# A hybrid attention and MLP block: the product with w_out read in single PSUM banks, its weighing on VectorE, two low parts by adding DMAs

## The chip, the cores and the metric

The kernel runs on one core of a Trainium2 chip. The metric is the device time of one execution in microseconds. A core has a matrix engine (TensorE, here PE), a vector engine (VectorE, DVE), a scalar engine (ScalarE, ACT), a general engine (GpSimd, POOL) and a queue engine (SyncE, SP) that issues most transfers. PE writes its results into PSUM, which has eight banks; one bank holds 128 x 512 float32. Everything else lies in SBUF, and the large arrays in DRAM. The engines run on their own and wait for each other by semaphores.

## The reference

One block of a network over 1024 tokens of 1024 channels: two linear attention branches, merged by gates, then a product with `w_out`, a norm and a residual sum, then a second norm and an MLP. What the change touches begins with `merged`:

```python
merged = jax.nn.sigmoid(m_a) * y_a + jax.nn.sigmoid(m_d) * y_d
x = x + gate1 * rms_norm(merged @ w_out, post_mix_w)

h2 = rms_norm(x, pre_mlp_w) * (1.0 + scale2) + shift2
y = jnp.square(jax.nn.relu(h2 @ mlp_w1)) @ mlp_w2
x = x + gate2 * rms_norm(y, post_mlp_w)
```

All of it is float32.

## The kernel before, in words

*Products.* A float32 operand is split into a high part (rounded to the type fp32r, by a copy on ACT) and a low part (the operand less its high part, by a subtraction on DVE). A product is three matmuls: high by high, high by low, low by high. Every matmul is 128 x 128 by 128 x 512. The large products are made by Winograd's form of Strassen's method: the operands are cut into four quadrants, and seven products P1 to P7 of sums of quadrants take the place of eight. The sums of the results are had by letting several products accumulate in the same PSUM bank, with reads in between.

*The product with w_out* (from `out_plan`, line 1752) multiplies `merged` (quadrants Z11 to Z22, tiles `U`, `z` and `xq`) by `w_out` (quadrants B11 to B22, tiles `wq` and `raw`). The seven products run in the order P2, P1, P6, P5, P3, P7, P4. Each has four banks j of 128 tokens; in each bank k runs over four slices of the inner dimension, the first two of pair 0 (`kp`), the last two of pair 1. So a product is 4 x 4 x 3 = 48 matmuls, 12 a bank, and one "tick" of the kernel's clock is 6 matmuls, half a bank. The high and low parts are `mH`, `mL` (of `merged`) and `wO` (of `w_out`); `a_cast`, `b_cast` make the high parts, `a_low`, `b_low` the low ones.

*PSUM.* Two pools share the eight banks: `pm` has two tiles of two banks each (`pmt()`), `pa` four tiles of one bank (`pat()`). P2 fills two `pm` tiles, P1 to P3 then two more (the same two buffers, when P2's have been read), P7 and P4 four `pa` tiles. The results are gathered in tiles `y`: P2's is copied by ACT (`copy_y`), P1's is added to it by DVE (`first_half`); that is the first column half of the first token half. The sums after P6 and P5 are copied for the second token half; the sum after P3 is the first token half's second column half (`second_half`). P7 and P4 are added into the copies (`add_y`).

*The norm behind it.* For each token half: `square` takes the sums of squares on ACT, `weigh` multiplies a gathered 128 x 1024 tile by a weight row `gw1` (the norm's weight times gate1; tile `gw`) on GpSimd, `norm1` works out the factor in eleven short DVE operations, `residual` adds the scaled rows to x (tiles `xr`), `square2` and `norm2` are the same for the second norm, and give `xh`. `turn` transposes `xh` on PE into a `pm` tile and scales it on ACT into the tiles `F`. Both token halves do this, the second one during pass 1.

*Pass 1* is the start of the MLP: 32 products `prod1` of 12 matmuls each, of the weight w1 (tiles `w`, loaded to `raw`) by the first half's `F` (split into `oB`), into banks `pa`.

*What sets the order.* The code hands each engine its instructions in a fixed order. Calls of `at`, `on` and `st` put an operation at a tick: `on(t, ...)` means t ticks after P2's start. An operation stands in its engine's queue where its tick comes due in the program, and runs when its inputs and its buffer are ready and what stands ahead of it is done; it may run long before its tick. So a tick sets an order, not a time. The tiles `wO` and `w` lie in eight buffers (`wt`), so that a cast waits for PE to finish with an older weight.

The profile gives line 38, where a helper records every operation, for all of them: they are told apart by their tiles.

Of the kernel before, what the change touches and what calls it, by code (L numbers as in the profile page):

```python
# [8 lines left out]
F32 = mybir.dt.float32  # L9
# [3 lines left out]
AF = mybir.ActivationFunctionType  # L13
ALU = mybir.AluOpType
# [36 lines left out]
def block_kernel(ctx: ExitStack, tc: tile.TileContext, x, c, ada_w, ada_b, pre_mix_w, post_mix_w,  # L51
# [28 lines left out]
    def pmt():  # L80
        return pm.tile([128, 1024], F32, tag="pm", name=nm("pm"))
# [1321 lines left out]
    def on(t, fn):  # L1403
        at(begin + t - clock[0], fn)
# [159 lines left out]
    def r2(ps):  # L1564
        return ps.rearrange("p (a b) -> p a b", a=2)
# [305 lines left out]

    def turn(hf, a, g):

        pt = pmt()
        for i in range(4):
            for e in range(2):
                T.transpose(pt[:, i * 256 + e * 128:i * 256 + e * 128 + 128],
                            xhs[4 * hf + a + e][:, (4 * g + i) * 128:(4 * g + i + 1) * 128], ident)
        for i in range(4):
            k = 4 * g + i  # L1880
            if F[hf][k // 2] is None:
                F[hf][k // 2] = pair_tile("F")
            A.activation(F[hf][k // 2][:, k % 2, a * 128:(a + 2) * 128], pt[:, i * 256:(i + 1) * 256], AF.Identity,
                         scale=am2[:, k:k + 1], bias=sh2[:, k:k + 1])

    NG = 16
# [94 lines left out]
    on(64, lambda: norm1(1, 0, 4))  # L1981
    for j in range(4):
        on(64 + j, lambda j=j: residual(1, j, 0))
        on(66 + j, lambda j=j: square2(1, j))
    on(71, lambda: norm2(1, 0, 4))
    for n in range(4):
        on(74 + n, lambda n=n: turn(1, n // 2 * 2, n % 2))

    psb, psc = None, None
    for p in ("P2", "P1", "P6", "P5", "P3", "P7", "P4"):  # L1990
        if p in ("P2", "P1"):
            psb = [pmt(), pmt()]
        elif p == "P7":
            psc = [pat() for _ in range(4)]
        for h in range(2):
            if p == "P1":
                at(5 + 4 * h, lambda h=h, ps=psb: first_half(h, ps[h]))
            elif p in ("P2", "P6", "P5"):
                key = {"P2": (0, 0, h), "P6": (1, 0, h), "P5": (1, 1, h)}[p]
                at(5 + 4 * h, lambda h=h, ps=psb, key=key: copy_y(key, ps[h]))  # L2000
        for j in range(4):
            if p == "P3":
                at(3 + 2 * j, lambda j=j, ps=psb: second_half(j, four(ps)[j]))
            elif p in ("P7", "P4"):
                at(3 + 2 * j, lambda j=j, ps=psc, c=int(p == "P7"): add_y((1, c, j // 2), j, ps[j]))
        out_product(p, psc if p in ("P7", "P4") else four(psb), p in ("P2", "P1", "P7"))


    def t_ops():
# [76 lines left out]
    for n, (g, k) in enumerate(PASS1):  # L2086
        if n + 2 < len(PASS1):
            prep_pass1(*PASS1[n + 2], 0)
        if n % 2 and n // 2 + 4 < NG:
            at(0, lambda n=n: load_pass1(n // 2 + 4))  # L2090
        if n == 22:
            load_pass2(0, [t4((128, 4, 256), p="raw", tag="sl") for _ in range(2)])
        elif n in (27, 30):
            at(0, lambda n=n: load_pass2(1 if n == 27 else 2))
        if n == 26:
            p0 = prep_pass2(0)
            for j in range(8):
                at(j, p0[j])
        if n == 30:
            p1 = prep_pass2(1)  # L2100
            for j in range(4):
                at(j, p1.pop(0))
        if n < 30:
            at(0, lambda: some(1))
            if n % 2:
                at(1, lambda: some(1))
        if n == len(PASS1) - 1:
            load_uy(0)
        if k == 0:
            acc1[g] = pat()  # L2110
            uy1[g] = pair_tile("uy", "sl" if 4 <= g < 10 and g % 3 else "w4")
# [348 lines left out]
```

## Time and profile before

| | |
|---|---|
| median of 3 runs | 1912.64 us (1911.64 to 1913.68) |
| the profiled execution | 1912.39 us |
| its span, from the first to the last instruction | 1910.6 us |
| mean granted clock of PE | 0.995 |
| busy: PE, DVE, ACT, POOL | 98%, 73%, 46%, 9% |

The span is divided into busy time of each engine; a matmul counts as busy with a modelled end, so that PE can be busy and still lose time at a low clock. The product with w_out starts at 1178.1 us of the span, pass 1 at 1275.1 us. The timeline lists the instructions of one engine in order of time, like ones merged, with the idle time before one in brackets and the operation that ended it.

### The profile page before, as it was taken

The page shows a single profiled execution, that of the slowest core. Times are in us where ns is not written, and L with a number is a line of the kernel's source. Part 1 is how long each engine was busy: PE and PEld are TensorE (multiplying, and loading weights), DVE is VectorE, ACT ScalarE, POOL GpSimd, SP SyncE. Part 2 cuts the span into 40 slices and gives each one's busy share as a digit, 9 for nine tenths or more (in the row PEclk, how much of TensorE's full clock was granted, in tenths as well). Part 3 has the DMA queues.
Part 4 walks back from the last instruction along what each step waited for, and adds up shares of the span by engine and source line. Part 5 has one row for each costly group of instructions (what it writes and reads, how often), then busy time and mean ns, then how long its engine had stood idle before and what let it go on. Part 6 is the DMA issues. An engine that isn't in the chain of part 4 may idle for free. (4 is left out here: it accounts for less than half of the span.)

```text
span 1910.6 us, 26421 instructions
## 1 busy us (share of the span) xinstructions
PE 1871.3 (98%) x10169; PEld 1567.8 (82%) x10169; DVE 1386.7 (73%) x2129; ACT 887.3 (46%) x1609; POOL 163.0 (9%) x140
## 2 busy tenths in 40 slices
PE   7999999999999999999999999889999999999998
PEld 5788888989888888888888888668888888888886
DVE  5664834968756666766788679976678786777887
ACT  5564324243333444444655653558644446433333
POOL 2120111010110000000101100120012120000001
PEclk9999999999999999999999999989999999999999
DMA  9695573223125444444957853326666758252425
GB/s 312 216 252 185 153 144 101 78 78 111 56 85 175 131 131 131 131 131 160 231 180 188 257 149 112 93 87 222 223 208 216 249 204 307 96 220 90 175 99 99
DMA packets 251230, 309.07 MB, mean 162 GB/s; under 512 B 72450, under 2 KB 178128, under 8 KB 251104
## 3 DMA queue, kind: packets, MB, share of 16 engines
q1 hardware_dynamic: 222464, 274.67, 45.1%
q0 software_dynamic: 12368, 17.70, 5.3%
q10 hardware_dynamic: 16272, 15.02, 2.4%
q8 instruction: 80, 1.31, 0.3%
q14 instruction: 46, 0.38, 0.1%
HBM read 226.95 MB, written 80.39 MB: 161 GB/s over the span
## 5 line engine op out<-in xcount | busy, mean ns | idle before, releaser
L38 PE MATMUL pm<-hH,wH 128*128 128x512 f32 x864 | 286.7, 413 | 0.0
L38 PE MATMUL pm<-hL,wH 128*128 128x512 f32 x864 | 268.6, 392 | 0.0
L38 PE MATMUL pm<-hH,wL 128*128 128x512 f32 x864 | 267.4, 391 | 0.0
L38 PE MATMUL pm<-oH,wB 128*128 128x512 f32 x672 | 214.5, 394 | 0.0
L38 PE MATMUL pa<-w,yH 128*128 128x512 f32 (+1 forms) x696 | 212.3, 387 | 0.0
L38 PEld LDWEIGHTS pm<-hL,wH 128*128 128x128 f32 x864 | 162.2, 188 | 36.5
L38 PEld LDWEIGHTS pm<-hH,wL 128*128 128x128 f32 x864 | 162.1, 188 | 36.4
L38 DVE TENSOR_TENSOR w<-raw,w 128x512 fp32r<-128x512 f32 (+1 forms) x144 | 129.3, 901 | 46.7 <-ACT w L38 46.1
L38 PEld LDWEIGHTS pm<-hH,wH 128*128 128x128 f32 x864 | 145.1, 190 | 17.0
L38 PEld LDWEIGHTS pa<-w,yH 128*128 128x128 f32 x696 | 130.1, 188 | 26.8 <-DVE ya L38 0.4
L38 PEld LDWEIGHTS pm<-oH,wB 128*128 128x128 f32 x672 | 126.2, 188 | 25.7
L38 ACT CAST w<-raw 128x512 fp32r<-128x512 f32 (+1 forms) x144 | 99.4, 711 | 88.6 <-DVE raw L38 79.4
L38 PE MATMUL pa<-w,yL 128*128 128x512 f32 (+1 forms) x348 | 134.5, 387 | 0.0
L38 PE MATMUL pm<-oL,wB 128*128 128x512 f32 x336 | 130.9, 390 | 0.0
L38 PE MATMUL pa<-oB,w 128*128 128x512 f32 x480 | 113.8, 395 | 5.0 <-DVE w L38 5.0
L38 PEld LDWEIGHTS pa<-oB,w 128*128 128x128 f32 x480 | 90.8, 190 | 25.0 <-DVE w L38 6.2
L38 ACT CAST wH<-raw 128x1024 fp32r<-128x1024 f32 x62 | 64.5, 1048 | 98.3 <-PE pm L38 55.9
L38 DVE SCALAR_TENSOR_TENSOR cv<-pm,ccol,cv 128x1023 f32<-128x1023 f32 (+2 forms) x72 | 92.1, 1279 | 13.7 <-ACT cv L38 12.3
L38 DVE TENSOR_TENSOR wL<-raw,wH 128x1024 fp32r<-128x1024 f32 x62 | 76.1, 1231 | 34.8 <-ACT wH L38 34.7
L38 PE MATMUL pm<-oT,w 128*128 128x512 f32 x384 | 90.8, 389 | 0.0
L38 PE MATMUL pa<-oT,w 128*128 128x512 f32 x384 | 90.8, 389 | 0.0
L38 DVE TENSOR_TENSOR ya<-pa,ya 128x512 f32<-128x512 f32 (+1 forms) x83 | 56.0, 683 | 43.6 <-PE pa L38 43.6
(398 smaller groups left out, 3759.5 us busy)
## 6 DMA issues: line engine op xcount, KB each, us to landing
yL<-y_d SPq DMA_DIRECT2D x53, 512.0 KB, 7.2
raw<-in_mlp_w_dram SPq DMA_DIRECT2D x23, 1024.0 KB, 6.3
raw<-in_w_in_dram SPq DMA_DIRECT2D x18, 1024.0 KB, 7.3
raw<-in_w_in_dram SPq DMA_DIRECT2D x32, 512.0 KB, 5.0
araw<-in_ada_w_dram SPq DMA_DIRECT2D x32, 512.0 KB, 3.8
raw<-in_mlp_w_dram SPq DMA_DIRECT2D x18, 512.0 KB, 5.6
araw<-in_ada_w_dram SPq DMA_DIRECT2D x32, 256.0 KB, 6.8
sl<-sg_d SPq DMA_DIRECT2D x16, 512.0 KB, 6.9
```

Source lines behind the costliest of these rows:

```text
L38: r = fn(*args, **kw)
```

## The change

Five things are changed, all between P2 of the product with w_out and the middle of pass 1:

- `weigh` runs on VectorE instead of GpSimd; of the first token half it stands ten ticks (h = 0) and eight ticks (h = 1) later.
- P2 has two `pm` tiles of its own (`psa`); P1, P6, P5 and P3 accumulate in four `pa` tiles (`psb`), P7 and P4 in two `pm` tiles (`psc`). So P1 and P3 are read bank by bank, P6 and P5 copied in two halves, and P7 and P4 added as 128 x 1024 instead of 128 x 512.
- The low parts of P2's and P1's weights are made as in `b_neg`: ACT writes the negative high part, and a DMA of GpSimd's queue adds the quadrant of w_out from DRAM.
- `turn` works on a `pa` tile: four transposes into one bank and two scalings, twice as many calls. The first half's stand 4 ticks (first pair) and 2 ticks (second pair) later, its splits 2 ticks; of the second half, the norm stands 2 to 6 ticks later and the transposes 5.
- In `out_plan` the sums Z12 and Z21 stand 3 and 5 ticks later, and some casts and low parts of P5 and P4 a tick or two off. The transposed sums of the MLP come 4 ticks later, and `uy` tiles use the pool `sl` from g = 7 instead of 4.

```diff
+    def b_neg(p, key, kp):
+        H, L = ww[p, kp]
+        A.activation(L, H.bitcast(F32), AF.Copy, scale=-1.0)
+        r0 = key[0] * 512 + kp * 256
+        G.dma_start(L, w_out[r0:r0 + 256, HALF[key[1]]].rearrange("(k p) c -> p k c", p=128), accum_op=ALU.add)
...
-                  (-11 + 4 * kp, b_cast, "P2", B21, kp), (-10 + 4 * kp, b_low, "P2", B21, kp),
+                  (-11 + 4 * kp, b_cast, "P2", B21, kp), (-10 + 4 * kp, b_neg, "P2", B21, kp),
...
-                  (-3 + 4 * kp, b_cast, "P1", B11, kp), (-2 + 4 * kp, b_low, "P1", B11, kp),
+                  (-3 + 4 * kp, b_cast, "P1", B11, kp), (-2 + 4 * kp, b_neg, "P1", B11, kp),
...
-                  (12 + kp, a_sum, Z12, Z12, Z11, kp), (14 + kp, a_sum, Z21, Z22, Z11, kp),
-                  (14 + kp, a_cast, "P5", "s1", kp), (16 + kp, a_low, "P5", "s1", kp),
+                  (15 + kp, a_sum, Z12, Z12, Z11, kp), (19 + kp, a_sum, Z21, Z22, Z11, kp),
+                  (13 + kp, a_cast, "P5", "s1", kp), (17 + kp, a_low, "P5", "s1", kp),
...
-        tt(G, y, y, gw1[:, HALF[c]].unsqueeze(1).to_broadcast([128, 2, 512]), mul)
+        tt(V, y, y, gw1[:, HALF[c]].unsqueeze(1).to_broadcast([128, 2, 512]), mul)
...
-        pt = pmt()
-        for i in range(4):
+        pt = pat()
+        for i in range(2):
...
-    def first_half(h, ps):
-        tt(V, Y[0, 0, h], r2(ps), Y[0, 0, h], add)
+    def first_half(j, ps):
+        y = Y[0, 0, j // 2][:, j % 2]
+        tt(V, y, ps, y, add)
...
+    def add_y(c, h, ps):
+        y = Y[1, c, h]
+        tt(V, y, r2(ps), y, add)
...
-        on(16 + 4 * h, lambda h=h: weigh(0, 0, h))
+        on(26 + 2 * h, lambda h=h: weigh(0, 0, h))
...
-    for a, t in ((0, 45), (2, 51)):
-        for g in range(2):
-            on(t + g, lambda a=a, g=g: turn(0, a, g))
+    for a, t in ((0, 49), (2, 53)):
+        for g in range(4):
+            on(t + g // 2, lambda a=a, g=g: turn(0, a, g))
...
-    for n in range(4):
-        on(74 + n, lambda n=n: turn(1, n // 2 * 2, n % 2))
+    for n in range(8):
+        on(79 + n // 2, lambda n=n: turn(1, n // 4 * 2, n % 4))
...
-    psb, psc = None, None
+    psa, psb, psc = [pmt(), pmt()], None, None
     for p in ("P2", "P1", "P6", "P5", "P3", "P7", "P4"):
-        if p in ("P2", "P1"):
-            psb = [pmt(), pmt()]
+        if p == "P1":
+            psb = [pat() for _ in range(4)]
         elif p == "P7":
-            psc = [pat() for _ in range(4)]
+            psc = [pmt(), pmt()]
```

How the order moves is seen at three places of DVE's queue. The first is the gather of the first half, at the end of P1 and the start of P6. Before (`wO` and `mL` are low parts for P6 and P5, `y` the gathered tile, `z` and `U` sums of quadrants of merged):

```order
L38 TENSOR_TENSOR wO_10621<-wq_10585,wO_10620 128x1024
L38 TENSOR_TENSOR wO_10634<-wq_10598,wO_10633 128x1024
L38 TENSOR_TENSOR z_9207<-z_9207,U_8740 128x1024
L38 TENSOR_TENSOR z_9262<-z_9262,U_8811 128x1024
L38 TENSOR_TENSOR y_10577<-pm_10612,y_10577 128x1024
L38 TENSOR_TENSOR U_8992<-U_9102,U_8740 128x1024
L38 TENSOR_TENSOR U_9048<-U_9144,U_8811 128x1024
L38 TENSOR_TENSOR mL_10666<-xq_10538,mH_10665 128x1024
L38 TENSOR_TENSOR mL_10679<-xq_10567,mH_10678 128x1024
L38 TENSOR_TENSOR y_10624<-pm_10613,y_10624 128x1024
```

With the change:

```order
L38 TENSOR_TENSOR wO_10627<-wq_10589,wO_10626 128x1024
L38 TENSOR_TENSOR wO_10640<-wq_10602,wO_10639 128x1024
L38 TENSOR_TENSOR y_10581<-pa_10616,y_10581 128x512
L38 TENSOR_TENSOR y_10581<-pa_10617,y_10581 128x512
L38 TENSOR_TENSOR z_9207<-z_9207,U_8740 128x1024
L38 TENSOR_TENSOR y_10630<-pa_10618,y_10630 128x512
L38 TENSOR_TENSOR z_9262<-z_9262,U_8811 128x1024
L38 TENSOR_TENSOR mL_10663<-xq_10541,mH_10662 128x1024
L38 TENSOR_TENSOR y_10630<-pa_10619,y_10630 128x512
```

The two gathers of 128 x 1024 have become four of 128 x 512, and the sums that stood ahead of the first one now stand behind it.

The second place is the start of P4, behind the first half's norm (`xh` is its result, `wO` the last low part for P4, `y` the results of P7, `cw` the next pair's norm). Before:

```order
L38 TENSOR_SCALAR xh_10873<-xr_10590,rs_10988 128x1024
L38 TENSOR_SCALAR xh_10889<-xr_10610,rs_10988 128x1024
L38 TENSOR_TENSOR wO_10966<-wq_10307,wO_10965 128x1024
L38 TENSOR_TENSOR y_10820<-pa_10941,y_10820 128x512
L38 TENSOR_TENSOR y_10820<-pa_10942,y_10820 128x512
L38 TENSOR_SCALAR cw_11068<-vb_10504 128x2
```

With the change:

```order
L38 TENSOR_SCALAR xh_10885<-xr_10594,rs_10998 128x1024
L38 TENSOR_SCALAR xh_10901<-xr_10614,rs_10998 128x1024
L38 TENSOR_TENSOR wO_10976<-wq_10307,wO_10975 128x1024
L38 TENSOR_TENSOR y_10830<-pm_10953,y_10830 128x1024
L38 TENSOR_SCALAR cw_11047<-vb_10507 128x2
```

The add of P7 has kept its place behind the norm, and is one operation on a tile of two banks.

The third place is the start of pass 1 (`w` are low parts of its weights, `oB` those of F, `gw` the weight row). Before:

```order
L38 TENSOR_TENSOR w_11130<-raw_10916,w_11130 128x512
L38 TENSOR_TENSOR oB_11159<-F_11033,oB_11158 128x1024
L38 TENSOR_TENSOR y_10742<-pa_10942,y_10742 128x512
L38 TENSOR_TENSOR oB_11170<-F_11036,oB_11169 128x1024
L38 TENSOR_TENSOR y_10781<-pa_10943,y_10781 128x512
L38 TENSOR_TENSOR oB_11189<-F_11056,oB_11188 128x1024
L38 TENSOR_TENSOR oB_11209<-F_11059,oB_11208 128x1024
L38 TENSOR_TENSOR y_10781<-pa_10944,y_10781 128x512
L38 TENSOR_TENSOR w_11204<-raw_10916,w_11204 128x512
L38 TENSOR_TENSOR w_11235<-raw_10936,w_11235 128x512
```

With the change:

```order
L38 TENSOR_TENSOR w_11126<-raw_10928,w_11126 128x512
L38 TENSOR_TENSOR y_10748<-pm_10953,y_10748 128x1024
L38 TENSOR_TENSOR oB_11185<-F_11081,oB_11184 128x1024
L38 TENSOR_TENSOR oB_11195<-F_11089,oB_11194 128x1024
L38 TENSOR_TENSOR y_10830<-y_10830,gw_9965 128x1024
L38 TENSOR_TENSOR y_10788<-pm_10954,y_10788 128x1024
L38 TENSOR_TENSOR w_11210<-raw_10928,w_11210 128x512
L38 TENSOR_TENSOR oB_11228<-F_11108,oB_11227 128x1024
L38 TENSOR_TENSOR y_10865<-y_10865,gw_9965 128x1024
L38 TENSOR_TENSOR oB_11245<-F_11116,oB_11244 128x1024
L38 TENSOR_TENSOR w_11241<-raw_10948,w_11241 128x512
L38 TENSOR_TENSOR y_10748<-y_10748,gw_9965 128x1024
```

The weighings of the second half now stand in DVE's queue, among the low parts that pass 1 waits for.

More of the change, by code (lines that the diff above doesn't have):

```diff
@@ L1772, in out_plan @@
                   (33 + kp, b_cast, "P7", B12, kp), (34 + kp, b_low, "P7", B12, kp),
-                  (41 + kp, b_cast, "P4", B21, kp), (42 + kp, b_low, "P4", B21, kp)]
+                  (41 + kp, b_cast, "P4", B21, kp), (41 + 4 * kp, b_low, "P4", B21, kp)]
         for t, fn, *a in sorted(r, key=lambda e: e[0]):
@@ L1872, in turn @@
     def turn(hf, a, g):
-        pt = pmt()
-        for i in range(4):
+        pt = pat()
+        for i in range(2):
             for e in range(2):
                 T.transpose(pt[:, i * 256 + e * 128:i * 256 + e * 128 + 128],
[L1878 to L1883, printed above, removed]
+                            xhs[4 * hf + a + e][:, (2 * g + i) * 128:(2 * g + i + 1) * 128], ident)
+        if F[hf][g] is None:
+            F[hf][g] = pair_tile("F")
+        for i in range(2):
+            k = 2 * g + i
+            A.activation(F[hf][g][:, i, a * 128:(a + 2) * 128], pt[:, i * 256:(i + 1) * 256], AF.Identity,
                          scale=am2[:, k:k + 1], bias=sh2[:, k:k + 1])
@@ L1935, in on, with copy_y, copy_first @@
         at(base + t - clock[0], fn)
-    def four(ps):
-        return [ps[j // 2][:, HALF[j % 2]] for j in range(4)]
-    def copy_y(key, ps):
+    def copy_y(key, h, ps):
         y = Y[key] = pair_tile("y")
+        for e in range(2):
+            A.copy(y[:, e], ps[2 * h + e])
+    def copy_first(h, ps):
+        y = Y[0, 0, h] = pair_tile("y")
         A.copy(y, r2(ps))
-    def add_y(key, j, ps):
-        y = Y[key][:, j % 2]
+    def first_half(j, ps):
+        y = Y[0, 0, j // 2][:, j % 2]
         tt(V, y, ps, y, add)
-    def first_half(h, ps):
-        tt(V, Y[0, 0, h], r2(ps), Y[0, 0, h], add)
     def second_half(j, ps):
@@ L1980, in block_kernel @@
         on((57, 58, 60, 61)[n], lambda c=c, h=h: weigh(1, c, h))
-    on(64, lambda: norm1(1, 0, 4))
+    on(66, lambda: norm1(1, 0, 4))
     for j in range(4):
-        on(64 + j, lambda j=j: residual(1, j, 0))
-        on(66 + j, lambda j=j: square2(1, j))
-    on(71, lambda: norm2(1, 0, 4))
-    for n in range(4):
-        on(74 + n, lambda n=n: turn(1, n // 2 * 2, n % 2))
-    psb, psc = None, None
+        on(67 + 2 * j, lambda j=j: residual(1, j, 0))
+        on(69 + 2 * j, lambda j=j: square2(1, j))
+    on(77, lambda: norm2(1, 0, 4))
+    for n in range(8):
+        on(79 + n // 2, lambda n=n: turn(1, n // 4 * 2, n % 4))
+    psa, psb, psc = [pmt(), pmt()], None, None
     for p in ("P2", "P1", "P6", "P5", "P3", "P7", "P4"):
-        if p in ("P2", "P1"):
-            psb = [pmt(), pmt()]
+        if p == "P1":
+            psb = [pat() for _ in range(4)]
         elif p == "P7":
-            psc = [pat() for _ in range(4)]
+            psc = [pmt(), pmt()]
         for h in range(2):
[L1996 to L2000, printed above, removed]
-        for j in range(4):
[L2002 to L2006, printed above, removed]
+            if p == "P2":
+                at(5 + 4 * h, lambda h=h: copy_first(h, psa[h]))
+            elif p in ("P6", "P5"):
+                at(5 + 4 * h, lambda h=h, c=int(p == "P5"): copy_y((1, c, h), h, psb))
+            elif p in ("P7", "P4"):
+                at(5 + 4 * h, lambda h=h, c=int(p == "P7"): add_y(c, h, psc[h]))
+        for j in range(4):
+            if p in ("P1", "P3"):
+                at(3 + 2 * j, lambda j=j, fn=first_half if p == "P1" else second_half: fn(j, psb[j]))
+        two = psa if p == "P2" else psc
+        out_product(p, psb if p in ("P1", "P6", "P5", "P3") else [two[j // 2][:, HALF[j % 2]] for j in range(4)],
+                    p in ("P2", "P1", "P7"))
     def t_ops():
@@ L2076, in load_uy @@
         LD.dma_start(uy[:, 1], y_d[g // 2][0, :, g % 2, :])
-    at(23, lambda: todo.extend(t_ops()))
+    at(27, lambda: todo.extend(t_ops()))
     PASS1 = [(0, 0)] + [e for g in range(NG - 1) for e in ((g + 1, 0), (g, 1))] + [(NG - 1, 1)]
@@ L2110, in block_kernel @@
             acc1[g] = pat()
-            uy1[g] = pair_tile("uy", "sl" if 4 <= g < 10 and g % 3 else "w4")
+            uy1[g] = pair_tile("uy", "sl" if 7 <= g < 10 and g % 3 else "w4")
             prod1(acc1[g], w1.pop((g, 0)), "B11", True)
```

4 lines of the change are left out of this document (2 added, 2 removed).

## The prediction

> **What bounds the kernel now.** I read the page first, then the timeline of TensorE (PE) from 1178 to 1345 us, where the product with w_out and the start of the MLP lie, then the timelines of VectorE (DVE), ScalarE (ACT) and GpSimd (POOL) over the same stretch. "Rows" are start, duration, engine, line, operation, out<-in, count, and in brackets the idle time before and what ended it.
>
> ```profile
> span 1910.6 us, 26421 instructions
> PE 1871.3 (98%) x10169; PEld 1567.8 (82%) x10169; DVE 1386.7 (73%) x2129; ACT 887.3 (46%) x1609; POOL 163.0 (9%) x140
> ...
> 1178.12 0.62 PE L38 MATMUL pm<-wO,mH 128*128 128x512 f32 x2
> ...
> 1184.81 0.73 PE L38 MATMUL pm<-wO,mH 128*128 128x512 f32 x2 [1.09 <-DVE U L38]
> ...
> 1197.32 0.73 PE L38 MATMUL pm<-wO,mH 128*128 128x512 f32 x2 [1.34 <-ACT y L38]
> ...
> 1204.36 0.73 PE L38 MATMUL pm<-wO,mH 128*128 128x512 f32 x2 [1.28 <-DVE y L38]
> ...
> 1232.47 0.74 PE L38 MATMUL pm<-wO,mH 128*128 128x512 f32 x2 [1.74 <-DVE y L38]
> ...
> 1241.34 1.22 PE L38 MATMUL pm<-wO,mH 128*128 128x512 f32 x2 [3.09 <-DVE y L38]
> ...
> 1244.84 0.40 PE L38 MATMUL pa<-wO,mL 128*128 128x512 f32 x1
> ...
> 1254.44 0.33 PE L38 MATMUL pm<-ident,xh 128*128 128x128 f32 x1 [3.05 <-DVE xh L38]
> ...
> 1258.84 1.03 PE L38 MATMUL pm<-ident,xh 128*128 128x128 f32 x8
> ...
> 1275.13 6.05 PE L38 MATMUL pa<-oB,w 128*128 128x512 f32 x26
> 1285.68 20.79 PE L38 MATMUL pa<-oB,w 128*128 128x512 f32 x82 [4.49 <-DVE w L38]
> 1306.31 1.10 PE L38 MATMUL pm<-ident,xh 128*128 128x128 f32 x8
> 1307.17 0.71 PE L38 MATMUL pa<-oB,w 128*128 128x512 f32 x2
> 1308.35 1.19 PE L38 MATMUL pa<-oB,w 128*128 128x512 f32 x4 [0.47 <-DVE w L38]
> ```
>
> PE is the bound: it has no idle time to speak of outside this stretch. So what the change is worth is the idle time here. Undisturbed, 26 matmuls take 6.05 us, of which the last one's modelled 0.39 is not spacing: (6.05 - 0.39) / 25 = 0.2264 us each. For the same reason 0.16 (0.39 less 0.23) is lost in each wait beside the bracket. The losses:
>
> - Four short waits (1.09, 1.34, 1.28, 1.74): 5.45 + 4 x 0.16 = 6.1 us.
> - 1241.34: 3.25; then nine matmuls to 1244.84 take 3.50 instead of 2.04, so 1.46 more at a low clock. 4.7 us.
> - 1254.44: 3.21; then eight transposes and six matmuls take 4.40 to 1258.84, normally 0.86 (1306.31 to 1307.17) and 1.36; 2.2 more. 5.4 us.
> - 1285.68: 4.65; then 82 matmuls take 20.40 where 81 spacings are 18.34; 2.1 more. 6.7 us.
> - 1308.35: 0.6 us.
>
> Together 23.5 us: the most that any change here can give.
>
> **The change, part by part.**
>
> *The weighing leaves GpSimd.*
>
> ```profile
> 1209.08 5.76 POOL L38 TENSOR_TENSOR y<-y,gw 128x1024 f32<-128x1024 f32 x2 [102.61 <-DMA gw<-gw_d]
> 1278.73 9.12 POOL L38 TENSOR_TENSOR y<-y,gw 128x1024 f32<-128x1024 f32 x3 [0.28 <-ACT xh L38]
> ...
> 1209.89 6.03 DVE L38 TENSOR_TENSOR wO<-raw,wO 128x1024 fp32r<-128x1024 f32 x2
> 1227.20 2.35 DVE L38 TENSOR_TENSOR mL<-U,mH 128x1024 fp32r<-128x1024 f32 x2
> 1276.35 6.51 DVE L38 TENSOR_TENSOR oB<-F,oB 128x1024 fp32r<-128x1024 f32 x2
> 1283.39 5.61 DVE L38 TENSOR_TENSOR w<-raw,w 128x512 fp32r<-128x512 f32 x3
> ```
>
> Two DVE subtractions of 128x1024 take 2.35 us (1.22 alone, the next one 1.13 after it), but 6.03 and 6.51 beside POOL's multiplications, and three half as long take 5.61 where about 1.9 is due. That is 3.7 + 4.2 + 3.7 = 11.6 us of DVE time given back. The six multiplications cost DVE at most 6 x 1.13 = 6.8. [...] The last stretch ends at 1289.0, and the PE wait before 1285.68 is for one of those w: with it go the 4.65 and the 2.1 behind it.
>
> *Adding DMAs for the low parts of P2 and P1.* Four DVE subtractions go (4.5 us); four ACT copies of -1 times the high part (1.05 us each, the wB row below) and four POOL DMAs of 512 KB come.
>
> ```profile
> 1183.54 1.22 DVE L38 TENSOR_TENSOR U<-pm,U 128x1024 f32<-128x1024 f32 x1
> 1203.08 1.22 DVE L38 TENSOR_TENSOR y<-pm,y 128x1024 f32<-128x1024 f32 x1
> ...
> 1085.66 1.06 ACT L38 ACTIVATE wB<-wB 128x1024 fp32r<-128x1024 f32 x1 [1.41 <-issue]
> 1087.01 1.30 POOL L38 DMA_DIRECT2D wB<-in_w_branch_gdn_dram  x1 [6.70 <-ACT wB L38]
> 1086.98 1.22 DVE L38 TENSOR_TENSOR wB<-wq,wB 128x1024 fp32r<-128x1024 f32 x1
> DMA to landing us min/median/max: 5.9/9.7/10.7
> 1167.25 1.06 ACT L38 CAST wO<-wq 128x1024 fp32r<-128x1024 f32 x1 [7.13 <-PE pm L38]
> 1178.13 1.06 ACT L38 CAST wO<-raw 128x1024 fp32r<-128x1024 f32 x1 [3.43 <-issue]
> 1086.00:1097.00 11.00, 11.00 (x51) 9.09 (x50) 6.66 (x6) 7.15 (x8) 2.58 (x2) 1.00 1.12 314
> 1168.00:1180.00 12.00, 12.00 (x55) 9.94 (x54) 11.86 (x11) 4.32 (x5) 0.00 (x0) 1.00 0.15 46
> ```
>
> DVE is full here (11.86 of 12 us), so work taken from ahead of an operation brings it forward. The read of U at 1183.54, which PE awaits at 1184.81, has three of the removed subtractions before it: 1183.54 - 3.4 = 1180.1, done 1181.4, needed at 1178.12 + 24 x 0.2264 = 1183.55. That wait goes. P1 now writes four single banks that nobody holds, so 1197.32 goes. The first gather y stood at 1203.08; four subtractions (4.5) and two sums (2.3) ahead of it go: 1196.3, with P6 due at 1178.12 + 96 x 0.2264 = 1199.9. That wait goes.
>
> The price is lateness. Each cast waits for a weight buffer that PE frees, so it does not move. P1's second: 1178.13, the new copy ends 2.0 later, POOL issues 0.3 after that (1086.72 to 1087.01), 1180.4. It lands 5.9 to 10.7 later, 1186.3 to 1191.1, and is read by P1's eighth matmul at 1178.12 + 55 x 0.2264 = 1190.6. P2's second, from 1167.25: 1175.5 to 1180.3 against 1179.7. So 0 to 0.6 us each. I take nothing: the 10.7 was the DMA issued at 1087.0, in a window with a DMA share of 1.12 (the column before the GB/s); the window in which P2's second one falls shows 0.15. POOL has nothing else queued here, and ACT, busy 4.32 of 12 us, hides its copies. SP's queue keeps its loads in order; only in pass 1 do three stores of finished rows move behind other stores and one load of weights that are needed four products later.
>
> *Single banks for the first half.* Both waits of P3 (1232.47, 1241.34) end with a read y of the bank just finished, while PE stands in the middle of the next bank: the two banks are one tile, and the matmuls on one half are made to wait for the read of the other. With a tile per bank nothing writes what the read holds, so both go, and the low clock after the second: 1.9 + 4.7.
>
> *What is late next.* P7 and P4 now share two-bank tiles: P4 may start only after DVE's add of P7, which stands behind the whole norm of the first half.
>
> ```profile
> 1234.18 0.60 ACT L38 ACTIVATE xh<-pm 128x512 f32<-128x512 f32 x1 [2.73 <-PE pm L38]
> 1234.90 0.69 DVE L38 TENSOR_TENSOR y<-pm,gw 128x512 f32<-128x512 f32 x1 [2.48 <-ACT xh L38]
> ...
> 1239.25 1.06 ACT L38 ACTIVATE xh<-xr 128x1024 f32<-128x1024 f32 x1 [0.21 <-ACT xh L38]
> ...
> 1240.30 1.03 ACT L38 CAST wO<-wq 128x1024 fp32r<-128x1024 f32 x1
> 1241.24 1.05 ACT L38 ACTIVATE xh<-xr 128x1024 f32<-128x1024 f32 x1
> ...
> 1245.02 0.69 DVE L38 TENSOR_TENSOR y<-pm,gw 128x512 f32<-128x512 f32 x1 [3.74 <-ACT xh L38]
> ...
> 1256.10 1.28 DVE L38 TENSOR_TENSOR y<-pa,y 128x512 f32<-128x512 f32 x2
> ...
> 1256.90 1.94 ACT L38 ACTIVATE F<-pm,sh,am 128x256 f32<-128x256 f32 x4 [5.25 <-PE pm L38]
> ```
>
> Without waits P3 starts at 1178.12 + 192 x 0.2264 = 1221.6 and its second bank is done at 1227.2. ACT squares it, DVE weighs it 0.72 later, 1227.95. From that y to the first square of xr is 4.35 (1234.90 to 1239.25), over a cast to the end of the second square 3.04, the square of the fourth bank and its y 0.72: fourth y at 1236.1. From there to the add is 11.08 (1245.02 to 1256.10), less 1.13 for a wO that now stands earlier: 1246.0, and 1.22 for the longer add, 1247.3. P4 is due at 1221.6 + 96 x 0.2264 = 1243.3. **New wait: 4.0 us**, and 1.8 at a low clock behind it, between the 1.46 and 2.2 above. The transposes that PE awaited at 1254.44 now come behind P4's first six matmuls, when xh is done: the 5.4 there go.
>
> *Later transposes, in single banks.* Pass 1's second matmul needs a low part of oB: from the first half's last two transposed banks ACT needs 1.94 for them (the four scalings of the 1256.90 row) and 1.05 for the cast, DVE 1.22: 4.2 us, while PE has the other four transposes (0.43), P4's last 12 matmuls (2.7) and one more (0.2): 3.3. So 0.9 late. Behind it DVE has two of the weighings and an add more (3.5 us), nearly all covered by two products of 12 matmuls (5.4); I take 0.4. The second half's transposes now share four banks with the accumulators: a visit of PE is 0.86 + 1.36 = 2.2, ACT needs 1.94 for its two banks, and among four visits stand five more ACT operations on 128x512, at most 0.6 each like the square at 1234.18: between nothing and 3.0 late; taken 1.2, a little under the middle, as some stand ahead of the first visit.
>
> Sum: 23.5 gone; 4.0 + 1.8 + 0.9 + 0.4 + 1.2 = 8.3 new; **gain 15.2 us**. The profiled execution took 1912.39 (span 1910.6), near the median of 1912.64: 1912.4 - 15.2 = 1897.2, called **1897**. Behind this stretch PE has no waits in the trace, so nothing absorbs the gain.
>
> **The rivals.**
>
> - *Adding DMAs land late.* If they take the 10.7 above, or 12 as with more traffic, P2 and P1 each wait up to 1.9 us: 1897 to 1901. Against it: the DMA shares. 10%.
> - *The new wait at P4 is longer,* through a DVE operation or buffer that the order doesn't show as late: at 7 us, 1900, with more behind it 1904. 10%.
> - *DVE's stretch isn't POOL's doing* and the weighing only adds 6.8 us to DVE; then the 6.7 at pass 1 stays: 1904. The three rows speak against it. 5%.
> - [...] 3%. [...]
> - *Better:* P4's wait is under 1 us: 1892. 2%.
>
> **How the numbers follow.** The forecast has 70%, within 1893 to 1900 by its own unknowns (P4's clock and the transposes). The range 1892 to 1903 leaves out the slow rival, the third and the tails, and holds 8 in 10. A measurement of this kernel tells 0.2% (3.8 us) from no change: faster 95% (all but the slow case and a sum of late cases), within 0.2% 2%, slower 3%.
>
> **What the changed profile would show.** Right: no PE wait between 1178 and 1243 us; one of some 4 us for DVE y near 1243, with slow matmuls behind; no POOL multiplication by gw, no DVE subtraction of 3 us; pass 1 starting near 1263 instead of 1275.1. Wrong: PE waits at its second or eighth matmul of P2 or P1 (DMAs); waits inside P3; a wait of several us at the transposes behind 1290; new idle time after 1320.

## The result, and the profile after

| | before | after |
|---|---|---|
| median | 1912.72 us (4 runs, 1911.64 to 1913.68) | 1896.04 us (4 runs, 1895.27 to 1896.71) |
| the profiled execution, its span | 1912.39, 1910.6 us | 1895.27, 1893.5 us |

The ratio is 0.9913, with a 95% interval of 0.9896 to 0.9930: 16.7 us faster, inside the range of 1892 to 1903 and 1 us from the forecast of 1897.

The page of the changed kernel, and its list of PE's waits (what waits for what: us in total, times, longest):

```profile
span 1893.5 us, 26430 instructions
PE 1865.9 (99%) x10169; PEld 1565.7 (83%) x10169; DVE 1377.3 (73%) x2129; ACT 892.1 (47%) x1617; POOL 151.6 (8%) x138
...
PE pm L38 <- DVE cw L38: 3.7, 1, 3.7
PE pa L38 <- DVE oB L38: 1.1, 2, 0.8
...
PE pa L38 <- ACT F L38: 0.5, 2, 0.3
```

Between P2's start and the end of the program PE has five waits left, where it had nine. Here they stand in PE's timeline, with what runs slowly behind the first:

```profile
1177.42 0.62 PE L38 MATMUL pm<-wO,mH 128*128 128x512 f32 x2
...
1242.47 0.39 PE L38 MATMUL pm<-wO,mL 128*128 128x512 f32 x1
1246.55 0.70 PE L38 MATMUL pm<-wO,mH 128*128 128x512 f32 x2 [3.69 <-DVE cw L38]
...
1248.06 1.91 PE L38 MATMUL pa<-ident,xh 128*128 128x128 f32 x8
...
1251.89 1.03 PE L38 MATMUL pa<-ident,xh 128*128 128x128 f32 x8
...
1262.75 0.45 PE L38 MATMUL pa<-oB,w 128*128 128x512 f32 x1
1263.96 7.09 PE L38 MATMUL pa<-oB,w 128*128 128x512 f32 x30 [0.76 <-DVE oB L38]
1271.37 24.57 PE L38 MATMUL pa<-oB,w 128*128 128x512 f32 x107 [0.32 <-DVE oB L38]
...
1303.47 0.66 PE L38 MATMUL pa<-ident,xh 128*128 128x128 f32 x4 [0.25 <-ACT F L38]
1304.38 25.91 PE L38 MATMUL pa<-oB,w 128*128 128x512 f32 x113 [0.25 <-ACT F L38]
```

The reader should see three things. There is no bracket between 1177.42 and 1242.47: all the waits of P2 to P3 are gone. The wait forecast at P4 is there, and eight transposes behind it take 1.91 us instead of 1.03. And pass 1 starts at 1262.75 instead of 1275.13.

VectorE's timeline over the same stretch:

```profile
1179.43 1.22 DVE L38 TENSOR_TENSOR U<-pm,U 128x1024 f32<-128x1024 f32 x1
...
1195.57 1.28 DVE L38 TENSOR_TENSOR y<-pa,y 128x512 f32<-128x512 f32 x2
...
1227.30 0.69 DVE L38 TENSOR_TENSOR y<-pa,gw 128x512 f32<-128x512 f32 x1 [1.40 <-ACT xh L38]
...
1242.72 1.42 DVE L38 TENSOR_SCALAR xh<-xr,rs 128x1024 f32<-128x1024 f32 x2
1244.05 1.22 DVE L38 TENSOR_TENSOR wO<-wq,wO 128x1024 fp32r<-128x1024 f32 x1
1245.19 1.22 DVE L38 TENSOR_TENSOR y<-pm,y 128x1024 f32<-128x1024 f32 x1
...
1262.68 2.36 DVE L38 TENSOR_TENSOR oB<-F,oB 128x1024 fp32r<-128x1024 f32 x2 [5.73 <-ACT oB L38]
```

The add of P7 at 1245.19 is what P4 waits for (the list names `cw`, the next DVE operation, which starts 0.1 us before that add's modelled end). It stands behind the norm's `xh` and a low part of `wO`. Two subtractions of `oB` take 2.36 us, no longer 6.51.

**A measure for the experiments.** Kernels that are the same up to P2 (the changed one, e5, e6, e7 and e11 below) start it anywhere between 1176.93 and 1180.19 us, 3.3 us apart, by stages that these experiments leave alone. (P2's weights, whose making the change touches too, are made ahead of that, from 1162 us on.) So beside the medians I use the *rest*: span less the start of P2 (first `wO` row of PE's timeline), of the one profiled execution. Before: 1910.6 - 1178.12 = 732.5 us. After: 1893.5 - 1177.42 = 716.1, and 717.6 in a second profile (e5). The change is worth 14.9 to 16.4 us there; 15.2 were forecast. As two profiles of one kernel are 1.5 us apart in it, a smaller difference of the rest says little by itself.

| kernel | median us | ratio to before (95%) | P2 starts | rest | rest against before |
|---|---|---|---|---|---|
| changed kernel | 1896.04 | 0.9913 (0.9896 to 0.9930) | 1177.42 | 716.1 | -16.4 |
| the same again (e5) | 1895.80 | 0.9922 (0.9909 to 0.9936) | 1178.92 | 717.6 | -14.9 |
| e1 weighing on DVE alone | 1909.60 | 0.9986 (0.9977 to 0.9995) | 1177.37 | 731.5 | -1.0 |
| e8 the same, issued later | 1905.27 | 0.9967 (0.9956 to 0.9978) | 1177.65 | 726.0 | -6.5 |
| e2 e1 and the adding DMAs | 1902.55 | 0.9957 (0.9944 to 0.9971) | 1179.59 | 724.5 | -8.0 |
| e9 single banks alone | 1908.29 | 0.9985 (0.9977 to 0.9994) | 1178.20 | 728.4 | -4.1 |
| e12 all but the later transposes | 1897.48 | 0.9927 (0.9914 to 0.9941) | 1177.86 | 717.6 | -14.8 |
| e3 changed, weighing on GpSimd | 1902.17 | 0.9948 (0.9936 to 0.9961) | 1177.95 | 722.0 | -10.5 |
| e4 changed, no adding DMAs | 1899.46 | 0.9937 (0.9924 to 0.9949) | 1176.36 | 719.9 | -12.5 |
| e10 changed, one DMA late | 1898.32 | 0.9930 (0.9917 to 0.9944) | 1179.27 | 718.0 | -14.5 |
| e6 changed, early add | 1891.47 | 0.9896 (0.9883 to 0.9910) | 1180.19 | 710.8 | -21.7 |
| e7 e6 and early split | 1889.87 | 0.9890 (0.9877 to 0.9904) | 1176.93 | 710.3 | -22.2 |
| e11 e7 and spread transposes | 1889.15 | 0.9888 (0.9874 to 0.9901) | 1177.99 | 709.1 | -23.4 |

### The profile page after: what moved, and what is told of

Read it like the earlier page. It is cut to its first block, busy times and chain, and to the rows that moved or that the text cites. A ratio compares the mean times of both kernels' runs of the same rounds, so it can differ in the third digit from the quotient of the medians.

```text
span 1893.5 us, 26430 instructions
## 1 busy us (share of the span) xinstructions
PE 1865.9 (99%) x10169; PEld 1565.7 (83%) x10169; DVE 1377.3 (73%) x2129; ACT 892.1 (47%) x1617; POOL 151.6 (8%) x138
```

## The experiments

**One part alone: the weighing (e1, e8).** To the kernel before:

```diff
-        tt(G, y, y, gw1[:, HALF[c]].unsqueeze(1).to_broadcast([128, 2, 512]), mul)
+        tt(V, y, y, gw1[:, HALF[c]].unsqueeze(1).to_broadcast([128, 2, 512]), mul)
```

> The kernel before with the weighing alone moved to VectorE. Theory (GpSimd's multiplications by gw stretch VectorE's subtractions, and this alone makes the wait at the start of pass 1): the wait for w before 1285.68 (4.65 and 2.1 at a low clock behind it) and the one of 0.6 at 1308.35 go, nothing else moves: 7.3 us less, about 1905.4 (1904 to 1907); the subtractions of oB take 2.35 us for two instead of 6.51. Rival (the stretch has another cause): VectorE only gets 6.8 us more work, the subtractions stay long, the wait stays or grows: 1912 to 1919.

It gained 2.1 us by the medians (before: 1911.67 in this set of runs). The start of pass 1 did what the theory said, as PE's and DVE's timelines of this run show: there is no wait for `w` in its first 88 matmuls, and no stretched subtraction. The later, short wait for `w`, which the theory let go too, is still there (0.47 us):

```profile
1279.59 20.59 PE L38 MATMUL pa<-oB,w 128*128 128x512 f32 x88
...
1306.61 1.21 PE L38 MATMUL pa<-oB,w 128*128 128x512 f32 x4 [0.47 <-DVE w L38]
...
1280.80 2.35 DVE L38 TENSOR_TENSOR oB<-F,oB 128x1024 fp32r<-128x1024 f32 x2
```

But a new wait stood at P6's third bank, where the kernel before has none. DVE's timeline of the same run, then PE's:

```profile
1208.56 1.23 DVE L38 TENSOR_TENSOR y<-y,gw 128x1024 f32<-128x1024 f32 x1 [1.61 <-DMA gw<-gw_d]
...
1210.84 1.22 DVE L38 TENSOR_TENSOR y<-pm,y 128x1024 f32<-128x1024 f32 x1
...
1203.60 0.72 PE L38 MATMUL pm<-wO,mH 128*128 128x512 f32 x2 [1.26 <-DVE y L38]
1212.11 1.22 PE L38 MATMUL pm<-wO,mH 128*128 128x512 f32 x2 [2.75 <-DVE y L38]
...
1237.18 0.74 PE L38 MATMUL pm<-wO,mH 128*128 128x512 f32 x2 [1.50 <-DVE y L38]
```

The first weighing waits 1.61 us for the row `gw`, and the second gather, which PE needs, stands behind it. From P6's start at 1203.60 to P3's wait at 1237.18 it is 33.6 us; the same stretch took 28.1 before (1204.36 to 1232.47). So 5.5 us are given back there in this profile: the wait and a low clock behind it (half of full for 6.8 us, as the last section shows). On GpSimd the same wait, the end of 102.61 us of idle time in the kernel before, had cost nothing, since nothing else was queued there: behind its two multiplications POOL's next instruction starts at 1276.04. So the second run took over the later places:

```diff
-        on(16 + 4 * h, lambda h=h: weigh(0, 0, h))
+        on(26 + 2 * h, lambda h=h: weigh(0, 0, h))
```

> The kernel before with the weighing on VectorE, and the first half's two weighings issued at 26 and 28 instead of 16 and 20, as the changed kernel has them. Theory (the first run lost 5.5 us at 1212 only because a weighing waited 1.6 us for gw ahead of VectorE's second gather): no wait at 1212, 7.3 us less than before, 1904 to 1906. Rival (VectorE has no room for the 2.3 us of these two weighings anywhere in this stretch): they lengthen the waits of P3 instead, 1906 to 1910.

5.5 us less than before by the medians (1910.72 in this set of runs) and 6.5 by the rest, near the 7.3, of which 0.6 was the short wait for `w` that stays here too; the wait at 1212 is gone. The move by ten ticks is therefore no detail: without it most of the weighing's gain is lost in the kernel before. In the changed kernel the early place was not tried.

**The weighing back on GpSimd in the changed kernel (e3).**

```diff
-        tt(V, y, y, gw1[:, HALF[c]].unsqueeze(1).to_broadcast([128, 2, 512]), mul)
+        tt(G, y, y, gw1[:, HALF[c]].unsqueeze(1).to_broadcast([128, 2, 512]), mul)
```

> The changed kernel with the weighing back on GpSimd. Theory: VectorE's subtractions of oB and w at the start of pass 1 are stretched again (about 8 us lost against 4.6 saved, and the two multiplications of the first half stretch others near 1217), PE waits at the first products of pass 1: 4 to 7 us more than the changed kernel, 1900 to 1903. Rival (the stretch is not GpSimd's doing): VectorE has 6.8 us less to do and the time is that of the changed kernel or up to 1 us less, 1895 to 1896.

6.1 us more by the medians, 4.4 to 5.9 by the rest. POOL's and DVE's timelines and PE's, all at pass 1:

```profile
1266.78 5.22 POOL L38 TENSOR_TENSOR y<-y,gw 128x1024 f32<-128x1024 f32 x2 [39.90 <-ACT xh L38]
...
1269.67 6.74 DVE L38 TENSOR_TENSOR oB<-F,oB 128x1024 fp32r<-128x1024 f32 x2
1276.33 4.09 DVE L38 TENSOR_TENSOR w<-raw,w 128x512 fp32r<-128x512 f32 x3
...
1273.14 1.65 PE L38 MATMUL pa<-oB,w 128*128 128x512 f32 x6 [1.52 <-DVE oB L38]
1276.46 1.89 PE L38 MATMUL pa<-oB,w 128*128 128x512 f32 x7 [1.67 <-DVE oB L38]
```

The stretch is back where the multiplications are back: 6.74 us for two subtractions that take 2.36 without them, and PE waits for them. The rival, that DVE would only have less to do, is out. Part of the loss is earlier: POOL's first two multiplications, from 1209.22, take 17.66 us (5.76 in the kernel before), two DVE subtractions beside them take 6.75 (from 1221.21), and the wait at P4 is 4.46 us instead of 3.69.

**The low parts back on DVE in the changed kernel (e4).**

```diff
-                  (-11 + 4 * kp, b_cast, "P2", B21, kp), (-10 + 4 * kp, b_neg, "P2", B21, kp),
+                  (-11 + 4 * kp, b_cast, "P2", B21, kp), (-10 + 4 * kp, b_low, "P2", B21, kp),
...
-                  (-3 + 4 * kp, b_cast, "P1", B11, kp), (-2 + 4 * kp, b_neg, "P1", B11, kp),
+                  (-3 + 4 * kp, b_cast, "P1", B11, kp), (-2 + 4 * kp, b_low, "P1", B11, kp),
```

> The changed kernel with the low parts of P2 and P1 subtracted by VectorE instead of made by adding DMAs. Theory: 3.4 us more stand ahead of the read of U and 4.5 ahead of the first gather; P2's third bank waits 1.3 us again and P6's start 0.3 to 1: 1897.3 to 1899. Rival (the single banks alone cured these waits and the DMAs are idle ornament): 1896 within 0.5.

3.4 us more by the medians, 2.4 to 3.9 by the rest, a little over the forecast. PE's timeline and one row of DVE's:

```profile
1183.05 0.73 PE L38 MATMUL pm<-wO,mH 128*128 128x512 f32 x2 [1.09 <-DVE U L38]
1199.88 0.70 PE L38 MATMUL pa<-wO,mH 128*128 128x512 f32 x2 [0.21 <-DVE y L38]
1248.53 1.19 PE L38 MATMUL pm<-wO,mH 128*128 128x512 f32 x2 [4.80 <-DVE cw L38]
...
1228.70 1.28 DVE L38 TENSOR_TENSOR y<-pa,gw 128x512 f32<-128x512 f32 x2
```

The two waits that the theory named are back, at 1.09 and 0.21. The third row was not expected: the wait at P4 grew by 1.1 us. It begins some 56 us after the last of these subtractions (1187.8 to 1243.7; the first is an estimate, 11.43 us after P2's start as in the kernel before). DVE's timeline of this run, from 1221.89, has no pause up to P3's first `y`. In the changed kernel it reaches the second `y` of P3 with 1.40 us to spare (the bracket at 1227.30 above); here it comes late to both (two in a row without a bracket), and the whole norm follows.

**The adding DMAs on the kernel before (e2).** e1's edit, and with `b_neg` as in the change:

```diff
-(-10 + 4 * kp, b_low, "P2", B21, kp)
+(-10 + 4 * kp, b_neg, "P2", B21, kp)
...
-(-2 + 4 * kp, b_low, "P1", B11, kp)
+(-2 + 4 * kp, b_neg, "P1", B11, kp)
```

> The kernel before with the weighing on VectorE and the adding DMAs for the low parts of P2 and P1; two-bank tiles and transposes as before. Theory (VectorE's four subtractions make the waits at P2's third bank and at the start of P6, while the wait at P1's third bank and the two in P3 are of the two-bank tiles): 1.25 and 1.44 go beside what the weighing gives: about 1902.7 (1901.5 to 1904.5), with waits left at P1's third bank, twice in P3, and at the transposes. Rival (the adding DMAs are worth nothing by themselves): the time of the run with the weighing alone. Rival (they land late): new waits of some us inside P2 or P1.

The median agrees with the forecast of 1902.7; by the rest it is 8.0 us less than before where 10.0 were forecast. Two errors cancel in part: e1's wait at P6's third bank is here too (2.86 us), and the wait at P1's third bank, which I had put down to the two-bank tile, is gone. Against e1 it is 7.0 us less, not the 2.7 by which the two forecasts differ. Part of that is the clock, which is half for 3.4 us behind P6's wait here and for 6.8 us in e1. ACT's timeline, of the kernel before and of this run, shows why:

```profile
1188.44 1.05 ACT L38 CAST mH<-U 128x1024 fp32r<-128x1024 f32 x1 [3.68 <-DVE U L38]
1196.26 1.00 ACT L38 COPY y<-pm 128x1024 f32<-128x1024 f32 x1
```

```profile
1186.52 1.06 ACT L38 CAST mH<-U 128x1024 fp32r<-128x1024 f32 x1 [0.27 <-DVE U L38]
1193.19 1.01 ACT L38 COPY y<-pm 128x1024 f32<-128x1024 f32 x1
```

ACT's copy of P2's second half stands behind casts that wait for DVE's `U`. With four subtractions less ahead of `U`, ACT copies 4.5 us sooner after P2's start (13.6 instead of 18.1 us), and P1 finds the banks free. That wait was DVE's backlog, handed on through ACT.

**The single banks alone (e9).** In the kernel before, P1 to P3 in four `pa` tiles:

```diff
-        if p in ("P2", "P1"):
-            psb = [pmt(), pmt()]
+        if p == "P2":
+            psb = [b for _ in range(2) for t_ in (pmt(),) for b in (t_[:, HALF[0]], t_[:, HALF[1]])]
+        elif p == "P1":
+            psb = [pat() for _ in range(4)]
```

(and the reads of P1 to P3 one bank each).

> The kernel before with P1, P6, P5 and P3 alone in four single banks, their reads by VectorE and ScalarE a bank each; weighing, subtractions, P7, P4 and transposes as before. Theory (the two-bank tile makes the waits at P1's third bank and in P3): the wait for ScalarE's y (1.33) and both waits in P3 (1.74, 3.09 and the low clock behind them) are gone; the waits for U (1.09) and at pass 1 (4.5) stay; the one at P6 is 1.3 to 2.2, as PE gets there earlier; the one at the transposes stays between 1 and 5 us: in all 6 to 8 us less than before, about 1904. Rival (VectorE's backlog makes these waits, whatever the tiles): PE still waits for VectorE's y in P3, 1909 to 1911.

The theory holds for P3: both waits are gone, while DVE is as late as before (it reads P3's first bank at 1231.98; before, at 1231.74). But the gain is 2.9 us (before: 1911.16 in this set; 4.1 by the rest), not 7. PE's and DVE's timelines:

```profile
1204.00 0.70 PE L38 MATMUL pa<-wO,mH 128*128 128x512 f32 x2 [2.45 <-DVE y L38]
1250.09 0.48 PE L38 MATMUL pm<-ident,xh 128*128 128x128 f32 x1 [6.13 <-DVE xh L38]
...
1210.09 6.08 DVE L38 TENSOR_TENSOR wO<-raw,wO 128x1024 fp32r<-128x1024 f32 x2
1231.98 1.28 DVE L38 TENSOR_TENSOR y<-pa,gw 128x512 f32<-128x512 f32 x2
```

The wait at P6 grows from 1.28 to 2.45, a little more than the forecast 1.3 to 2.2. PE now reaches the transposes 7.4 us earlier (1250.09 - 6.13 against 1254.44 - 3.05), the norm's `xh` only 4.35 earlier (1249.28 against 1253.63), since its first two `y` still stand behind the stretched subtractions. The wait there grows from 3.05 to 6.13. This part pays in full only when the others have moved DVE's chain too.

**All but the later transposes (e12).** e9, e8 and the adding DMAs together; transposes, P7, P4 and the order of the sums as before.

> All of the change but its last part: weighing on VectorE at 26 and 28, adding DMAs, single banks for P1, P6, P5 and P3; the transposes, P7's and P4's single banks and the order of the sums as in the kernel before. Theory (the norm of the first half is the bound behind P3, and the last part of the change only moves where PE meets it, from the transposes to P4): no wait before the transposes; there PE arrives 30 matmuls into P7, near 1238.6 where xh comes near 1243.4, and waits 4.8 us with 1.8 at a low clock behind it, then 0.6 for w later: the time of the changed kernel within 1.5 us, 1894.5 to 1897.5. Rival (the later transposes earn a share of their own): 2 to 6 us more than the changed kernel, 1898 to 1902, with waits of more than 7 us at the transposes or a new one at pass 1.

1897.48 us, at the edge of what the theory allowed: 1.4 to 1.7 us more than the changed kernel by the medians, 0.1 to 1.6 by the rest, which the intervals of the two ratios do not separate. Ahead of pass 1's rows PE waits only at the transposes:

```profile
1245.11 0.48 PE L38 MATMUL pm<-ident,xh 128*128 128x128 f32 x1 [5.89 <-DVE xh L38]
```

So the later transposes, with what goes with them, earn little by themselves: PE meets the same norm 5.89 us early at the transposes, or 3.7 us early at P4. What they do take away is the short wait for `w`, 0.48 us here, which the changed kernel does not have.

**One adding DMA made later (e10).** In the changed kernel, so that ACT copies P2's first half ahead of it:

```diff
-(-2 + 4 * kp, b_neg, "P1", B11, kp)
+(-2 + 7.5 * kp, b_neg, "P1", B11, kp)
```

> The changed kernel with the second adding DMA of P1 made later: its ScalarE copy stands behind ScalarE's copy of P2's first two banks. Theory (in the changed kernel it lands near 1188.3 and PE needs it near 1189.9, so 1.6 us of margin): the copy starts near 1184.0, the DMA near 1185.1, it lands near 1193.6, and PE waits some 3.7 us at P1's eighth matmul, with 0 to 1.8 at a low clock behind it: 1899.5 to 1901.5. Rival (the landing has more margin than the rows of the profile say): 1896 to 1897.

It cost 2.3 us by the medians and 1.2 of rest at the mean of the changed kernel's two: between the theory and its rival. POOL's issue in the changed kernel, with the DMA view's row for it (KB, us from issue to landing), then the same of this run and PE's wait:

```profile
1179.84 1.20 POOL L38 DMA_DIRECT2D wO<-in_w_out_dram  x1 [3.42 <-ACT wO L38]
...
wO<-in_w_out_dram POOLq DMA_DIRECT2D x1, 512.0 KB, 8.5
```

```profile
1187.19 1.20 POOL L38 DMA_DIRECT2D wO<-in_w_out_dram  x1 [8.91 <-ACT wO L38]
...
wO<-in_w_out_dram POOLq DMA_DIRECT2D x1, 512.0 KB, 6.2
...
1193.40 0.50 PE L38 MATMUL pa<-wO,mH 128*128 128x512 f32 x1 [1.50 <-DMA wO<-in_w_out_dram]
```

From P2's start the DMA is issued at 2.4 us in the changed kernel and at 7.9 here, 5.5 later, and PE waits 1.7 (1.50 and the 0.16). It landed 2.3 us quicker, so 1.5 us were margin. That agrees with its place: landed at 10.9 us after P2's start, needed at 55 x 0.2264 = 12.4.

**The wait at P4 (e6, e7, e11).** In the changed kernel, P7's first add and the last low part of P4 ahead of the norm that they stood behind:

```diff
-                  (41 + kp, b_cast, "P4", B21, kp), (41 + 4 * kp, b_low, "P4", B21, kp)]
+                  (41 + kp, b_cast, "P4", B21, kp), (41 + 5 * kp, b_low, "P4", B21, kp)]
...
-    for a, t in ((0, 42), (2, 47)):
+    for a, t in ((0, 47), (2, 50)):
         on(t, lambda a=a: norm2(0, a, 2))
-    for a, t in ((0, 49), (2, 53)):
+    for a, t in ((0, 51), (2, 53)):
```

> The changed kernel once more, unchanged, beside the next three on one chip: 1895 to 1897 by every theory.

> The changed kernel with VectorE's first add of P7 put ahead of the second norm of the first half's first rows (and of the last low part of w_out), the second add ahead of the second norm of the other rows, and the first transposes two ticks later. Theory (the one wait left, 3.85 us at P4 with 1.8 at a low clock behind it, is only the place of that add in VectorE's order): the add ends near 1242.0, P4 is due near 1242.7, no wait: 5.6 us less than the changed kernel, about 1890.5 (1889.5 to 1892). Rival (the norm is the real bound): the wait moves to the transposes, as xh now comes 1 to 2.4 us later: 1892 to 1895. Rival (P4 waits for the last low part of w_out next): 1.5 us left, 1892.

4.3 us less than the changed kernel on the same chip by the medians, 5.3 and 6.8 by the rest. No wait for P7's add is left, none moved to the transposes. DVE's add and the start of P4:

```profile
1243.53 1.22 DVE L38 TENSOR_TENSOR y<-pm,y 128x1024 f32<-128x1024 f32 x1
...
1245.47 0.62 PE L38 MATMUL pm<-wO,mH 128*128 128x512 f32 x2
```

The add ends 0.7 us ahead of P4. Then, ahead of ACT's last four scalings:

```diff
-        on(55 + kp, lambda kp=kp: split_op("B11", F[0][0:2], (kp,)))
+        on(53.5 + kp / 4, lambda kp=kp: split_op("B11", F[0][0:2], (kp,)))
```

> The same, and the split of B11 (ScalarE's casts and VectorE's low parts that pass 1 reads first) ahead of ScalarE's scalings of the last four transposed blocks, which B11 does not need. Theory: the wait of 0.98 at pass 1's second matmul goes, as the casts start some 1.9 us earlier: 1 us less than without, about 1889.5. Rival (B21 comes later by as much, or the accumulators wait for the banks that ScalarE frees later): the same as without, or up to 1 us more.

1.6 us less by the medians, 0.5 by the rest: the wait at pass 1's second matmul is gone, the one for the next `oB` grew from 0.32 to 0.61. B21 did not come later, as the rival had it: counted from P2's start, its low part begins 0.5 us sooner (86.6 instead of 87.1), but PE is there 0.8 us sooner. At last the second half's transposes, one call in a tick, with the sums behind them four ticks later:

```diff
-        on(79 + n // 2, lambda n=n: turn(1, n // 4 * 2, n % 4))
+        on(79 + n, lambda n=n: turn(1, n // 4 * 2, n % 4))
...
-    at(27, lambda: todo.extend(t_ops()))
+    at(31, lambda: todo.extend(t_ops()))
```

> The fastest kernel so far (the early add with the early split of B11), and the second half's eight visits of four transposes one tick apart instead of two in each tick, with what follows them four ticks later. Theory (two visits in a tick are faster than ScalarE's scaling of their banks): the two waits of 0.25 for F go, with 0.16 each: 0.8 us less in the profile, 1889 to 1889.9. Rival (each visit costs PE its own change between transposes and products): 0 to 1 us more.

0.7 us less by the medians, 1.2 by the rest, and both waits for `F` are gone. The ranges of e6, e7 and e11 overlap, so that these two steps gain is read from the waits that go. This is the fastest kernel of the study: 1889.15 us (1888.81 to 1890.49), 22 us below before in the same set of runs (1911.16) and some 7 below the changed kernel.

## Why the prediction was right, point by point

| term of the sum | forecast us | measured in the changed kernel |
|---|---|---|
| waits of before, with the low clock behind them | 23.5 gone | all gone; no PE wait up to 1242 |
| the read of U, after P2's start | 2.0 | 2.0 (1179.43 - 1177.42) |
| the first gather, after P2's start | 18.2 | 18.15 (1195.57 - 1177.42) |
| wait at P4 | 4.0 | 3.85 (1246.55 - 1242.47 - 0.23) |
| low clock behind it | 1.8 | 1.8 (1246.55 to 1251.89 is 5.34 for eight transposes and twelve matmuls, due 0.86 + 2.72); 2.95 in e5, where the same sum is 6.53 |
| pass 1's second matmul | 0.9 | 0.98 (1263.96 - 1262.75 - 0.23) |
| first products behind the weighings | 0.4 | 0.48 (0.32 and 0.16) |
| second half's transposes | 1.2 | 0.8 (two waits of 0.25, with 0.16 each); spreading them took 1.2 off the rest (e11) |
| gain | 15.2 | 16.4 and 14.9 by the rest |

- **The low clock, 1.8:** its size was luck, as two profiles of the changed kernel gave 1.8 and 2.95. The 2.2 that bounded it from above is also misread: it holds a second wait of 0.33 us for `xh`, at 1255.11 in the kernel before.
- **POOL's multiplications stretch DVE:** shown from both sides. Without them two subtractions of `oB` take 2.35 us (e1; 6.51 before), and e8 gains 6.5 us by the rest; with them they take 6.74 (e3; 2.36 in the changed kernel).
- **The two-bank tiles make the waits in P3:** shown by e9, where both (1.74 and 3.09 us) go although DVE is no earlier (1231.98 against 1231.74).
- **P1's third bank:** the prediction gave it to the tiles alone. e2 shows that the adding DMAs cure it too, through ACT, whose copy comes 13.6 instead of 18.1 us after P2's start. The sum was not touched, as both are in the change.
- **The adding DMAs, nothing for lateness:** right, with 1.5 us of margin by e10. The slow case that the range leaves out (3%) is shown by no run. The window with P1's second one in the changed kernel (DVE and POOL are the third and the fifth pair):

```profile
1178.00:1190.00 12.00, 12.00 (x55) 9.93 (x54) 11.93 (x12) 4.63 (x5) 1.20 (x1) 1.00 0.74 169
```

  DVE was busy 11.93 of 12 us, and POOL's issue took 1.20 and landed 8.5 us after it began.
- **The new wait is the norm in DVE's order:** shown by e6, which takes it away (3.69 us in the changed kernel) by order alone.

What the prediction didn't see: it quoted the row in which POOL's first weighing waits for `gw`, and did not ask what that wait would hold up on DVE. The later place in the code answered it; e1 lost 5.5 us without it. Here the sum came out right though the prediction had not worked it out. And it summed the parts. The sum was right for the whole change, but the single banks alone (e9) gave 4.1 us of rest, not the 8.1 of their waits (1.5 in P1, 1.9 and 4.7 in P3): a part by itself lets PE run ahead to the next thing that DVE's chain makes late.

## What to carry to other kernels

When one engine is the bound and another is full behind it, follow the full engine's order from one wait to the next. A wait that goes lets the bound engine arrive earlier at the next read of the same chain (in e9 PE was 7.4 us earlier at the transposes, and its wait there grew from 3.05 to 6.13), so sum the whole path and don't price parts alone. When work moves to a busier engine, look at what its first instruction waited for on the old one: there the wait was free, here all that is queued behind it waits too (in e1, 1.61 us for `gw` and 5.5 us lost).

## What the runs showed of the hardware

**The clock was half for 3.4 us or for 6.8, from no fixed point of a wait.** Windows of the changed kernel, of e5 (the same kernel) and of e1; the third column from the end is PE's granted clock:

```profile
1248.20:1251.00 2.80, 2.80 (x12) 2.56 (x11) 2.60 (x4) 1.85 (x5) 0.00 (x0) 0.50 0.77 316
```

```profile
1247.20:1253.60 6.40, 5.54 (x17) 4.68 (x18) 4.81 (x14) 1.75 (x4) 0.00 (x0) 0.50 0.77 294
```

```profile
1209.40:1211.20 1.80, 0.00 (x0) 0.00 (x0) 1.80 (x3) 0.00 (x0) 0.00 (x0) 1.00 0.00 0
...
1211.60:1218.00 6.40, 5.89 (x14) 4.64 (x15) 6.40 (x7) 5.07 (x8) 0.00 (x0) 0.50 0.01 3
```

Read in windows of 0.4 us, the clock is below full from 1247.8 to 1251.4 in the changed kernel, from 1246.9 to 1254.1 in e5 and from 1211.2 to 1218.4 in e1; the first and the last of these windows hold it in part (0.69 and 0.54, 0.94 and 0.53, 0.81 and 0.65), the others have 0.50. That makes 3.4, 6.8 and 6.8 us at half. So with the same wait of 3.7 us at P4, the clock was half for some 3.4 us after PE had resumed in one execution (PE resumed at 1246.55), and for some 6.8 us from within the wait in the other (PE resumed at 1248.06). In e1 it fell after about 2 us of idle time (PE's last matmul ends at 1209.36, the clock is still full up to 1211.2); behind a wait of 3.02 us in e2 it did not fall at all (the window from 1242.50 to 1248.50 has 1.00). So in these runs a wait of 3.0 to 3.7 us cost itself and between nothing (e2) and 2.95 us (e5) more. What sets the clock is not shown by these runs.
